# TensorE's instructions may pass at most six emitted ahead of them

## The chip, the cores and the metric

The kernel runs on one core of a Trainium2 chip as a single program. The metric is the device time of an execution in microseconds; a lower one is better. The engines are called as in the profile: PE is TensorE's matmul, PEld its weight load, DVE is VectorE, ACT is ScalarE, POOL is GpSimd and SP is SyncE.

## The reference

Two transformer-like blocks work on one sequence of 1024 positions of width 1024, all in 32-bit floats.

```
first_block:
  x = x + hybrid_mixer(rmsnorm(x))          # spatial gating, gated delta rule over 16 chunks
  x = x + memory_cross_attention(rmsnorm(x), rmsnorm(mem))
  x = x + square(relu(rmsnorm(x) @ w1)) @ w2          # 1024 -> 4096 -> 1024
  x = rmsnorm(x)
second_block:
  z = rmsnorm(x) @ w_in                               # split into nine parts
  y_pool  = windowed mean (2, 4, 8, 16) minus z, times pool_w
  y_sconv = s_b * conv3(s_c * s_h)
  y_conf  = silu(layernorm(conv31(c_a * sigmoid(c_g))))
  y_attn  = differential attention: softmax(q1 k1) - lam * softmax(q2 k2), times v
  x = x + concat(y_pool, y_sconv, y_conf, y_attn) @ w_out
  x = x + (silu(h @ w_gate) * (h @ w_up)) @ w_down    # h = rmsnorm(x)
```

## The kernel before, in words

Every product of two 32-bit matrices is made of three products of a rounded form: high times high, high times low and low times high. So each operand has two tiles, and the names end in h and l (hh and hl, wh and wl, b2h and b2l, th and tl, yh and yl). ACT makes the high tile by a copy into the rounded type; DVE, for weights POOL, makes the low tile as the difference. A PE instruction takes 128 x 128 weights against up to 512 columns. The activations stay in SBUF with features on partitions, and the weights stream in from memory as wr (or pr).

The stages follow each other: the mixer with a scan over 16 chunks (tiles pa, pb, st, vn), into which products for the memory's keys and values (gm) are woven as filling; cross attention; the first MLP; the second block's projection w_in with pooling, two convolutions and differential attention beside it; its projection w_out; the second MLP. In both MLPs the up products are made in pairs by a scheme with seven instead of eight block products; q is such a product's accumulator, b1, b2h, b2l, th and tl are its activations, ph, pl, wh, wl and p4 its weights, and pt, pu, pc and ft are what DVE and ACT make of q. fhh and fhl are the operands of the down product that follows (gm).

In the second block's projection the names are: stk, bh, bl and as for the attention's scores, amx for their maximum, ap for the softmax, apt and aT for its transpose, apo and ao for its product with v, yaT and yat for its result; tb and crb for a row spread over all partitions; cy for the 31-tap convolution; zp, pl, pld and pp for pooling (the last sum of a half is split: 64 partitions by DVE, a copy of the other 64 by POOL); gm_2301, gm_2316 and gm_2323 are output blocks of w_in, gm_2329 and gm_2361 the first two of w_out, with yh and yl from the four parts of the concatenation.

The order comes about in two steps. First the kernel itself is a set of tasks (generators). `drive` takes, at every step, the task of the best priority whose operands are ready by the kernel's own clock model, and lets it emit a few instructions. The framework's scheduler then orders each engine's instructions by a cost model of its own and adds the semaphores and the buffers' waits. The class `Eng` wraps an engine's instruction calls: it gives each instruction an ordering dependency, without a semaphore, on the one emitted a fixed number of places before it on the same engine. So the scheduler may lift an instruction over as many others at most. That number is in the table `_w` in line 203: 8 for ACT, SP and POOL, 24 for DVE. PE has no entry, so its number is 0, and its instructions may be lifted over any distance as far as their data allow. All instructions are emitted in line 210, inside that wrapper, which is why every row of the profile has line L210 and is told apart by its tiles.

Of the kernel before, what the change touches and what calls it, by code (L numbers as in the profile page):

```python
# [74 lines left out]
class Event:  # L75

    def __init__(self):
        self.done = False
        self.aps = []
# [119 lines left out]
class Eng:  # L199
    def __init__(self, eng, name, clock, tc):  # L200
        self._e, self._n, self._c, self._tc = eng, name, clock, tc
        self._past = []
        self._w = {"scalar": 8, "vector": 24, "sync": 8, "gpsimd": 8}.get(name, 0)

    def __getattr__(self, op):
        f = getattr(self._e, op)
# [2265 lines left out]
```

## Time and profile before

| what | value |
|---|---|
| time of three runs | 2617.35, 2618.58, 2618.97 us; median 2618.58 |
| profiled execution | 2613.1 us, span 2611.2 us |
| PE busy | 2499.2 us, 96% of the span, 11880 matmuls |
| DVE, ACT, POOL busy | 1563.7, 855.6, 820.5 us |
| mean granted clock of TensorE | 0.983 |

The profile comes from one execution. Busy times are added up for each engine; a wait belongs to the instruction behind it and names what ended it last. The granted clock is 1 at 2.4 GHz and 0.5 at 1.2 GHz. Times of a timeline are counted from the span's start.

### The profile page before, as it was taken

To read this page: it belongs to the slowest core of one execution; us is meant where nothing else is said; L and a number is where in the kernel's file an instruction comes from. 1 tells how busy PE (TensorE), PEld (TensorE's weight loads), DVE (VectorE), ACT (ScalarE), POOL (GpSimd) and SP (SyncE) were. 2 spreads that over 40 slices of the span, in tenths; PEclk is the share of its full clock that TensorE was granted. 3 is DMA by queue.
4 is the path that set the end of the run, shared out by engine and by line. 5 is a ranking of instruction groups with operands and counts; after the bars stand their busy time and mean duration, and the time that the engine had idled before them with its cause. 6 is when DMAs were issued, how large, how long until landed. Compare 5 with 4: busy or idle time off the path is not lost.

```text
span 2611.2 us, 30369 instructions
## 1 busy us (share of the span) xinstructions
PE 2499.2 (96%) x11880; PEld 2057.4 (79%) x11880; DVE 1563.7 (60%) x2316; ACT 855.6 (33%) x1220; POOL 820.5 (31%) x349
## 2 busy tenths in 40 slices
PE   8999999999989999999999798988989999999999
PEld 6788877888877888778888587776867888887887
DVE  7873767554457665553434857976676665664433
ACT  6422343333343333321213423434452222222210
POOL 1122121211244454322222421121245656662221
PEclk9999999999999999999999898999989999999999
DMA  3223156421132333542211232143222222236212
GB/s 130 77 77 94 63 173 207 171 89 49 65 129 82 120 105 121 227 145 99 98 57 49 97 105 57 41 145 93 85 81 73 81 89 89 65 128 235 81 49 89
DMA packets 99134, 268.25 MB, mean 103 GB/s; under 512 B 19976, under 2 KB 34480, under 8 KB 98992
## 3 DMA queue, kind: packets, MB, share of 16 engines
q1 hardware_dynamic: 78400, 192.40, 21.5%
q10 hardware_dynamic: 20592, 73.93, 8.5%
q8 instruction: 93, 1.52, 0.2%
q14 instruction: 49, 0.40, 0.1%
HBM read 196.55 MB, written 69.74 MB: 102 GB/s over the span
## 4 chain that ended last, share of the span: by engine, by line
PE 81%; DVE 11%; DMA 3%; issue 2%; ACT 2%; POOL 1%; SPq 0%; ACTq 0%; POOLq 0%; DVEq 0%
PE gm L210 46%; PE q L210 26%; DVE cy L210 1%; PE apo L210 1%; PE xs L210 1%; PE as L210 1%; PE xo L210 1%; DVE rq L210 1%; DVE ry L210 1%; DMA stk<-qkd 1%; POOL wl L210 1%; PE pk L210 1%; PE pb L210 1%; PE apt L210 1%; DVE sb L210 1%
## 5 line engine op out<-in xcount | busy, mean ns | idle before, releaser
L210 POOL TENSOR_TENSOR wl<-wr,wh 128x1024 fp32r<-128x1024 f32 (+1 forms) x137 | 339.7, 2481 | 1354.0 <-ACT wh L210 1302.2
L210 DVE TENSOR_TENSOR x<-gm,x 128x512 f32<-128x512 f32 x304 | 208.9, 688 | 346.2 <-PE gm L210 345.5
L210 ACT ACTIVATE wh<-wr 128x1024 fp32r<-128x1024 f32 (+2 forms) x147 | 153.2, 1042 | 621.7 <-PE gm L210 589.5
L210 PE MATMUL gm<-fhh,wh 128*128 128x512 f32 x864 | 337.6, 391 | 5.3 <-ACT fhh L210 4.6
L210 PE MATMUL gm<-fhl,wh 128*128 128x512 f32 x864 | 336.9, 390 | 1.0 <-DVE fhl L210 1.0
L210 PE MATMUL gm<-fhh,wl 128*128 128x512 f32 x864 | 336.6, 390 | 0.0
L210 PE MATMUL gm<-hh,wh 128*128 128x512 f32 x800 | 324.6, 406 | 11.5 <-ACT hh L210 7.3
L210 PE MATMUL gm<-hl,wh 128*128 128x512 f32 x800 | 318.3, 398 | 0.5 <-DVE hl L210 0.5
L210 PE MATMUL gm<-hh,wl 128*128 128x512 f32 x800 | 316.7, 396 | 0.0
L210 PEld LDWEIGHTS gm<-fhh,wh 128*128 128x128 f32 x864 | 162.2, 188 | 42.7 <-ACT fhh L210 5.4
L210 PEld LDWEIGHTS gm<-fhl,wh 128*128 128x128 f32 x864 | 162.3, 188 | 35.3 <-DVE fhl L210 2.2
L210 PEld LDWEIGHTS gm<-fhh,wl 128*128 128x128 f32 x864 | 162.3, 188 | 33.9
L210 PEld LDWEIGHTS gm<-hh,wh 128*128 128x128 f32 x800 | 152.9, 191 | 43.1 <-ACT hh L210 8.3
L210 PEld LDWEIGHTS gm<-hh,wl 128*128 128x128 f32 x800 | 152.7, 191 | 32.4 <-issue 0.5
L210 PEld LDWEIGHTS gm<-hl,wh 128*128 128x128 f32 x800 | 153.2, 191 | 31.4 <-DVE hl L210 1.9
L210 POOL TENSOR_TENSOR wl<-pr,wh 128x1024 fp32r<-128x1024 f32 x37 | 88.7, 2398 | 118.7 <-ACT wh L210 118.7
L210 POOL TENSOR_TENSOR wl<-sa,wh 128x1024 fp32r<-128x1024 f32 x37 | 89.1, 2409 | 107.3 <-ACT wh L210 104.3
L210 POOL TENSOR_TENSOR pl<-sb,ph 128x1024 fp32r<-128x1024 f32 x38 | 92.0, 2421 | 81.0 <-ACT ph L210 81.0
L210 PE MATMUL q<-th,wh 128*128 128x512 f32 x296 | 116.8, 395 | 0.0
L210 PE MATMUL q<-th,wl 128*128 128x512 f32 x296 | 116.3, 393 | 0.0
L210 PE MATMUL q<-tl,wh 128*128 128x512 f32 x296 | 116.2, 392 | 0.0
L210 PE MATMUL q<-th,p 128*128 128x512 f32 x304 | 103.5, 402 | 3.2 <-DVE pc L210 3.2
(461 smaller groups left out, 5233.6 us busy)
## 6 DMA issues: line engine op xcount, KB each, us to landing
fhr<-hd SPq DMA_DIRECT2D x54, 512.0 KB, 5.0
wr<-in_w_in_dram ACTq DMA_DIRECT2D x39, 512.0 KB, 3.5
xd<-x SPq DMA_DIRECT2D x32, 512.0 KB, 2.6
x<-xd SPq DMA_DIRECT2D x32, 512.0 KB, 5.4
pr<-in_ffn_w_dram SPq DMA_DIRECT2D x32, 512.0 KB, 3.6
wr<-in_ffn_w_dram ACTq DMA_DIRECT2D x32, 512.0 KB, 3.5
hd<-ft SPq DMA_DIRECT2D x27, 512.0 KB, 5.0
hd<-pc SPq DMA_DIRECT2D x27, 512.0 KB, 5.7
```

What stands on the lines that cost most here:

```text
L210: ins = f(*args, **kw)
```

## The change

One entry is added to the table of line 203, so that PE's instructions get the same ordering dependencies as those of the other engines, over six places. What is computed, the number of instructions and their emission stay as they are. The order on PE differs in 108 pieces (1454 lines of difference), on DVE in 33, on ACT in 17, on POOL in 3 and on SP in 2, since the scheduler places those engines' work by what PE does.

```diff
 class Eng:
     def __init__(self, eng, name, clock, tc):
         self._e, self._n, self._c, self._tc = eng, name, clock, tc
         self._past = []
-        self._w = {"scalar": 8, "vector": 24, "sync": 8, "gpsimd": 8}.get(name, 0)
+        self._w = {"tensor": 6, "scalar": 8, "vector": 24, "sync": 8, "gpsimd": 8}.get(name, 0)
```

The first place is on PE near the end of the second block's w_in (about 1735 to 1752 us in the trace of before): yaT are transposes of the attention's result, tb spreads the row ry, gm_2301 is an output block of 24 products. A + row stands there in the changed order, a - row only in that of before.

```order
 L210 MATMUL yaT_2302_12862<-cst_75,ao_1965_11196 128x128 x4
 L210 MATMUL yaT_2303_12868<-cst_75,ao_1965_11196 128x128 x4
+L210 MATMUL tb_2306_12882<-cst_75,ry_2273_12746 128x128 x4
+L210 MATMUL tb_2307_12889<-cst_75,ry_2273_12746 128x128 x4
 L210 MATMUL gm_2301_12858<-hh_1820_10437,wh_2248_12617 128x512
 L210 MATMUL gm_2301_12858<-hl_1821_10438,wh_2248_12617 128x512
```

Further on, at the end of gm_2301:

```order
 L210 MATMUL gm_2301_12858<-hh_1865_10683,wl_2249_12618 128x512
-L210 MATMUL as_2330_13012<-stk_2295_12841,stk_2294_12838 128x128
-L210 MATMUL as_2330_13012<-bh_1532_8648,idr_10693 128x128
-L210 MATMUL as_2330_13012<-bl_1533_8649,idr_10693 128x128
-L210 MATMUL as_2342_13049<-stk_2295_12841,stk_2294_12838 128x256
-L210 MATMUL as_2342_13049<-bh_1532_8648,idr_10693 128x256
-L210 MATMUL as_2342_13049<-bl_1533_8649,idr_10693 128x256
-L210 MATMUL tb_2306_12882<-cst_75,ry_2273_12746 128x128 x4
 L210 MATMUL gm_2316_12931<-hh_1816_10403,wh_2280_12766 128x512
-L210 MATMUL tb_2307_12889<-cst_75,ry_2273_12746 128x128 x4
 L210 MATMUL gm_2316_12931<-hl_1817_10404,wh_2280_12766 128x512
```

The two tb have moved from behind gm_2301 to ahead of it, and six score products as have gone from between the blocks gm_2301 and gm_2316 to a place behind gm_2323.

The second place is ACT at the same point of the program; wh_2313 is the high tile of a weight of w_out, crb is the evacuation of tb, wr are loads of weights. Before:

```order
L210 DMA wr_2315_12929<-in_w_out_2a_dram 128x768
L210 ACTIVATE wh_2313_12925<-wr_2282_12770 128x768
L210 ACTIVATE yat_2293_12837<-yaT_2302_12862,gv_76 128x512
L210 ACTIVATE yat_2293_12837<-yaT_2303_12868,gv_76 128x512
L210 DMA wr_2328_13009<-in_w_out_2a_dram 128x768
L210 ACTIVATE crb_2305_12881<-tb_2306_12882 128x512
L210 ACTIVATE crb_2305_12881<-tb_2307_12889 128x512
```

Now:

```order
L210 DMA wr_2315_12929<-in_w_out_2a_dram 128x768
L210 ACTIVATE yat_2293_12837<-yaT_2302_12862,gv_76 128x512
L210 ACTIVATE yat_2293_12837<-yaT_2303_12868,gv_76 128x512
L210 ACTIVATE crb_2305_12881<-tb_2306_12882 128x512
L210 ACTIVATE crb_2305_12881<-tb_2307_12889 128x512
L210 ACT_TABLE_LOAD
L210 ACTIVATE cy_2028_11573<-cy_2028_11573,gv_76 128x1024
L210 ACTIVATE cy_2240_12596<-cy_2240_12596,gv_76 128x1024
L210 ACTIVATE wh_2313_12925<-wr_2282_12770 128x768
L210 DMA wr_2328_13009<-in_w_out_2a_dram 128x768
```

wh_2313 and the load wr_2328 stood ahead of crb and the two cy, and stand behind them now.

The third place is PE at the start of the second MLP (about 1935 to 1950 us): q_2704 is the last product of the first pair, with the weight p4 as its last operand, q_2717 is the first product of the second pair and q_2718 the next.

```order
 L210 MATMUL q_2704_14439<-tl_2695_14387,p4_2605_14128 128x512
 L210 MATMUL q_2704_14439<-th_2694_14386,p4_2605_14128 128x512
+L210 MATMUL q_2717_14487<-b1_2601_14110,wh_2697_14410 128x512 x2
+L210 MATMUL q_2717_14487<-b1_2601_14110,wl_2698_14411 128x512
+L210 MATMUL q_2717_14487<-b1_2615_14158,wh_2697_14410 128x512 x2
+L210 MATMUL q_2717_14487<-b1_2615_14158,wl_2698_14411 128x512
+L210 MATMUL q_2717_14487<-b1_2633_14216,wh_2697_14410 128x512 x2
+L210 MATMUL q_2717_14487<-b1_2633_14216,wl_2698_14411 128x512
+L210 MATMUL q_2717_14487<-b1_2657_14285,wh_2697_14410 128x512 x2
+L210 MATMUL q_2717_14487<-b1_2657_14285,wl_2698_14411 128x512
 L210 MATMUL q_2718_14501<-th_2622_14182,wh_2702_14435 128x512
```

Twelve products of q_2717 (eight rows, four of them standing for two products each) stood among those of the first pair and follow it now.

## Rows read from the trace of the kernel before

**Rows 1.** Page: busy us (share of span) by engine; chain that ended last.
```profile
PE 2499.2 (96%) x11880; PEld 2057.4 (79%) x11880; DVE 1563.7 (60%) x2316; ACT 855.6 (33%) x1220; POOL 820.5 (31%) x349
...
PE 81%; DVE 11%; DMA 3%; issue 2%; ACT 2%; POOL 1%; SPq 0%; ACTq 0%; POOLq 0%; DVEq 0%
```

**Rows 2.** The waits of PE: engine, tile waiting <- releaser: us, times, longest.
```profile
PE zn L210 <- ACT zsq L210: 13.8, 1, 13.8
PE apt L210 <- DVE ap L210: 10.5, 6, 3.4
...
PE gm L210 <- DVE x L210: 4.8, 4, 1.6
...
PE pa L210 <- DVE st L210: 3.3, 3, 2.2
...
PE wsum L210 <- POOL wsT L210: 2.5, 1, 2.5
...
PE cm L210 <- DVE rq L210: 1.5, 1, 1.5
```

**Rows 3.** Windows: length, busy us of PE, PEld, DVE, ACT, POOL; granted clock; DMA share, GB/s.
```profile
1536.00:1712.00 176.00, 161.06 (x817) 135.79 (x818) 148.87 (x230) 66.88 (x132) 32.52 (x12) 0.95 0.18 57
1747.20:1789.50 42.30, 32.40 (x135) 24.41 (x135) 27.49 (x40) 19.45 (x35) 6.63 (x4) 0.88 0.53 161
```

**Rows 4.** Timeline of PE, 1747-1790: start, length, operation, [idle before <- releaser].
```profile
1749.03 0.30 PE L210 MATMUL as<-stk,stk 128*128 128x128 f32 x1 [1.80 <-DMA stk<-qkd]
...
1769.55 2.04 PE L210 MATMUL pp<-pld,wp 128*128 128x512 f32 x2 [5.50 <-DVE pld L210]
...
1784.72 0.50 PE L210 MATMUL gm<-yl,wh 128*128 128x512 f32 x1 [1.82 <-DVE yl L210]
```

**Rows 5.** Timeline of DVE, the same stretch.
```profile
1752.68 2.36 DVE L210 TENSOR_TENSOR cy<-cy,crb 128x1024 f32<-128x1024 f32 x2 [4.72 <-ACT crb L210]
...
1757.68 1.21 DVE L210 TENSOR_TENSOR pl<-pl 128x1020 f32<-128x1020 f32 x1
1763.69 0.42 DVE L210 TENSOR_REDUCE amx<-as 128x2 f32<-128x256 f32 x1 [4.80 <-PE as L210]
...
1764.22 2.82 DVE L210 TENSOR_TENSOR pl<-pl 64x1016 f32<-64x1016 f32 x1
...
1775.42 0.17 DVE L210 TENSOR_TENSOR pld<-pl,zp 128x16 f32<-128x16 f32 x1
...
1784.59 1.22 DVE L210 TENSOR_TENSOR yl<-py,yh 128x1024 fp32r<-128x1024 f32 x1
```

**Rows 6.** Timeline of ACT, the same stretch.
```profile
1747.05 0.84 ACT L210 ACTIVATE wh<-wr 128x768 fp32r<-128x768 f32 x1 [7.93 <-PE gm L210]
...
1776.30 0.37 ACT L210 ACTIVATE ap<-as,amx 128x128 f32<-128x128 f32 x1
```

**Rows 7.** Timeline of POOL, the same stretch.
```profile
1764.15 1.82 POOL L210 TENSOR_TENSOR wl<-wr,wh 128x768 fp32r<-128x768 f32 x1 [14.38 <-PE as L210]
```

**Rows 8.** Timeline of PE, start of the first MLP.
```profile
779.82 0.50 PE L210 MATMUL q<-b2h,ph 128*128 128x512 f32 x1 [4.51 <-ACT ph L210]
...
783.49 0.79 PE L210 MATMUL q<-b2h,pl 128*128 128x512 f32 x1 [1.51 <-POOL pl L210]
```

**Rows 9.** Timeline of PE, end of the first MLP's products.
```profile
1091.32 1.22 PE L210 MATMUL gm<-fhh,wh 128*128 128x512 f32 x2 [3.67 <-ACT fhh L210]
```

**Rows 10.** Timeline of DVE, the same place.
```profile
1092.44 0.68 DVE L210 TENSOR_TENSOR pc<-q,pu 128x512 f32<-128x512 f32 x1
```

**Rows 11.** Timeline of PE, end of the second MLP's products.
```profile
2351.20 0.50 PE L210 MATMUL q<-b2h,wh 128*128 128x512 f32 x1 [1.62 <-ACT pt L210]
```

**Rows 12.** Timeline of PE, start of the second MLP.
```profile
1945.00 0.50 PE L210 MATMUL q<-tl,ph 128*128 128x512 f32 x1 [0.76 <-DVE tl L210]
...
1948.96 0.80 PE L210 MATMUL q<-th,p 128*128 128x512 f32 x1 [3.22 <-DVE pc L210]
```

**Rows 13.** Timeline of DVE, the same place.
```profile
1929.93 1.23 DVE L210 TENSOR_TENSOR b2l<-xg,b2h 128x1024 fp32r<-128x1024 f32 x1 [0.72 <-ACT sq L210]
```

## The prediction

> **What bounds the kernel now.** I read the page first, then the waits of PE, then the timeline of each place where PE stands still. PE is busy for 2499.2 of 2611.2 us, 96%, and the chain that ended last is 81% PE; DVE, with 60% busy, holds 11% of that chain [rows 1]. The number of products does not change, so the change can win or lose only in the 112 us in which PE stands, in products that run at the lower clock after a stand, and nowhere else. The waits name 13.8 us at zn, 10.5 at apt, 5.5 at pp [rows 2, 4] and a tail of one to five microseconds each. A product costs 2499.2 / 11880 = 0.21 us on average [rows 1].
>
> In program order PE gets the products as the kernel's own planner emits them. The scheduler behind it then lifts products whose operands it believes to be ready past others, over any distance. From now on it may lift one over six others at most. So two things happen at each place. A product with a late operand that was lifted too far no longer stops PE there (a gain), and ready products that were lifted into a wait no longer fill it (a loss). On PE 108 pieces of the order differ. I went through the ones that lie at a wait. Negative numbers are time saved.
>
> **The pool place, 1747 to 1789: -5.** These 42.30 us hold 32.40 us of busy PE at a granted clock of 0.88 [rows 3]: PE waits 1.80 for a transfer of stk, 5.50 for pld and 1.82 for yl [rows 4]; 0.78 is left for one more wait. The 5.50 is a chain over three engines. On ACT, wh waits 7.93 us for the products of gm to give its buffer free and starts at 1747.05 [rows 6]. Behind it stand the two copies crb, for which DVE waits 4.72 us until 1752.68 [rows 5]. The pool sums on DVE come only after that; they then stand behind the score maximum amx, for which DVE waits 4.80 us until 1763.69, and the last sum of the first half takes 2.82 us [rows 5]. In the new order tb stands right behind yaT, that is ahead of the 24 products of gm_2301, wh stands behind crb and cy on ACT, and amx behind both halves of the pool on DVE.
> I follow the chain. crb is there some 4 us earlier, so cy's 2.36 us end near 1749. The first half then needs, from the rows' starts, 1752.68 + 2.36 to 1758.89 (3.9) and 1764.22 to about 1769.4, just ahead of PE's start at 1769.55 [rows 4] (5.2), less 0.7 for amx between them: 8.4 us and 0.7 for zp, so pld is ready near 1758.5. PE gets there about 1760, after its 72 products without the 1.80 wait, and the 5.50 goes. The second half ran from about 1769.4 to 1775.6 [rows 5], 6.2 us; it now starts behind gm_2323, near 1759.5, and ends near 1765.7. Then comes what was not late before: amx (1.1), the exponentials on ACT, which began at 1776.30 [rows 6], and from there to the end of the last yl at 1784.59 + 1.22 = 1785.8 [rows 5] 9.5 us of ACT and DVE. From 1766.8 that gives 1776.3. Behind the last yl PE now has the second output half, gm_2361, still to do: 18 products (3.8), 12 score products and the transposes (about 3), where before all but some of them lay in front. So the place ends at 1783.3 + 0.7 = 1784 and not at 1789.5: 5.5 saved, less half a microsecond for a product or two more at the low clock. The bounds: -9, if half of gm_2361 fits into the gap before yl as its six places allow and wl meets no sum of the pool; -1, if the chain from amx to yl grows as long as what is saved ahead of it.
>
> Of the three engines, DVE and GpSimd meet here. The 2.82 us sum runs beside wl on POOL, 1764.15 to 1765.97 [rows 5, 7]; a sum of the same size took 1.21 at 1757.68 with POOL idle [rows 5]. The Trainium skill, page SBUF — State Buffer, section "SBUF: two separate sides", calls the port pair of VectorE and GpSimd an exclusive lock that one holds for a whole instruction. The row agrees: 1.82 + 1.21 = 3.03 with a start 0.07 later and an end close to it. That rule speaks against this change, and it is a rival below.
>
> **Start of the first MLP, 776 to 790: -2 (-3.5 to 0).** PE waits 4.51 for ph and 1.51 for pl [rows 8], since ten products of q_1121 were lifted ahead of the second half of q_1116, whose operands are older. They go back behind it. The 6.0 us of waits go, but what stood ahead of them had been the filler and the next operands (pl ends on POOL near 783.5) are no earlier: a third is saved.
>
> **Ends of both MLPs' products: +1 (-0.5 to 2) and +2 (0 to 3).** At 1087.6 PE waits 3.67 for fhh [rows 9] and then runs four products of the next stage. Now the twelve products with p4 stand first. They need pc, which DVE starts at 1092.44 and ends 0.68 later [rows 10], behind fhl. So PE stands until 1093.1 and not 1091.3, and the four products (0.21 each, about 1.8 with the low clock) come after: 1.8 us of wait more, of which the four products' slower first run gives back 0.8. At 2351.20 PE waits 1.62 for pt [rows 11] after eight products that were lifted in front of it; they go behind: 8 x 0.21 = 1.7 more of wait, and 0.3 for the same pattern with pc at the end.
>
> **Start of the second MLP, 1917 to 1950: +1.5 (-1.5 to 9.3).** 23 products of four later results were lifted ahead of a product that waits for b1_2657, 4.8 us, and 12 products of q_2717 ahead of those with p4, 2.5 us. The end of this place is set by operands: tl, for which PE waits until 1945.00, and pc, for which it waits 3.22 until 1948.96 [rows 12]. b2l is ready at 1929.93 + 1.23 = 1931.2 [rows 13]. From there PE has 48 products, 48 x 0.21 = 10.1 us, or 13 with some at the low clock: 1941.3 to 1944. That is still ahead of 1945, so the 23 cost nothing. The 12 of q_2717 come after p4 and are lost, +2.5; a microsecond of earlier x from the pool place goes against it. Without the cover all 7.3 are lost, and 2 more at the low clock.
>
> **The differential attention, 1536 to 1712: 0 (-4 to +4).** The scores and transposes move back to where they are emitted. apt waits 10.5 us for ap in six places [rows 2], mostly here. But DVE is busy for 148.87 of 176 us [rows 3], with convolution taps and softmax in an order that hardly changes; PE's waits shift from one of its products to another.
>
> **Small places.** Scan (343 to 462): the wait for st, 2.2 at its longest [rows 2], gets six products as cover, others come later: -1.5 (-4 to 2). Start: the 2.5 for wsT go [rows 2], twelve products now run earlier at DVE's pace: +1 (-0.5 to 3). A projection at 680 no longer runs ahead of xt: +1 (0 to 2.5). Before zn (13.8 [rows 2]): cs and tb are a little earlier, the chain of small DVE operations that zn waits for stays: -1 (-2.3 to 1). csum stands ahead of wl on POOL, so cm's 1.5 goes [rows 2]: -1.5 (-2 to 1). One of the four waits for x, 4.8 / 4 = 1.2 [rows 2], goes: -1.2 (-1.4 to 0). All pieces that I did not follow, some ninety, can hardly gain where PE does not wait: +1.5 (0 to 8).
>
> **The sum.** -5 - 2 + 1 + 2 + 1.5 + 0 - 1.5 + 1 + 1 - 1 - 1.5 - 1.2 + 1.5 = -4.2. The profiled execution took 2613.1 us (span 2611.2 and 1.9 around it), so it would take 2608.9. The median of the three runs is 2618.58, 5.5 above the profiled one; the difference is carried to it: 2618.6 - 4.2 = 2614.4.
>
> **Rivals.**
> The gain is larger. The waits at apt and zn shrink with the order too, because DVE and ACT get their inputs in the order in which their own lists ask for them. For it: the pool place shows one engine's queue held by another's lifted product [rows 5, 6]. Against it: DVE is 85% busy in the attention [rows 3]. With -9 at the pool place and -3 in the attention the sum is -11.2: 2607.4.
> The gain is eaten by the port. In the new order wl_2314 falls on the first sums of the pool, the copy of pl on the last one, and wl_2327 on the second half. One such meeting cost 2.82 - 1.21 = 1.6 [rows 5], and the forecast has one in it; two more make the sum -4.2 + 3.2 = -1.0: 2617.6. By the skill's lock it would be nearly the same, since each holds for a whole wl of 1.82.
> Slower: PE stands at the first late operand of the second MLP. Place: 1917 to 1950. The lifted 23 + 12 products are not regained, because b2l or th come no earlier and the 48 products behind run at the low clock past 1945. Price: 9.3 in place of 1.5, and the end of the second MLP's products at its upper bound, 3 in place of 2: -4.2 + 7.8 + 1 = +4.6; with 2 more in the unfollowed pieces, which have the same pattern, +6.6, 2625.2. It decides when the 48 products end after 1945. For it: PE is the bound nearly everywhere, so every product not lifted costs its time. Against it: the row for pc shows that the end is set elsewhere.
>
> **Chances.** The forecast 0.40 (its own range 2609 to 2620), the larger gain 0.22, the port 0.15, slower 0.23. About 0.2% of the time, 5.2 us, is what a measurement can tell from no change; the line for faster is 2613.4. Half of the forecast's case lies below it: faster 0.20 + 0.22 = 0.42; same 0.20 + 0.15 = 0.35; slower 0.23. For 8 in 10 the range goes from 2604 to 2625.
>
> **What would show it.** Right: the pool place is 4 to 6 us shorter, its wait at pp is gone, and PE now waits several microseconds in front of yl; the wait for ph at 780 and that of cm for rq are gone; a wait for pc of over 4 us at 1093. Wrong: a wait at pp that stays near 5 us; more than 2 us of new wait at b1 or th near 1924 to 1945; a larger sum at apt; or a new wait in a place that I did not follow.

## The result: 1.2% slower, and where the time went

The changed kernel takes 2649.97 us (median of 4 runs, 2648.74 to 2651.66); beside it the kernel before took 2617.97. The ratio is 1.0124, with a 95% interval of [1.0111, 1.0137], and the difference 32.0 us. The forecast was 4.2 us in the other direction, with a range that ended at 2625. Here and below a difference in us is one of medians; the ratios are estimated from all runs and differ from the ratio of the medians by about 0.001 at most.

The page of the changed kernel, busy time and chain, is the answer to [rows 1]:

```profile
PE 2504.0 (95%) x11880; PEld 2062.2 (78%) x11880; DVE 1569.5 (59%) x2316; ACT 857.5 (32%) x1220; POOL 822.0 (31%) x349
...
PE 79%; DVE 13%; ACT 3%; issue 2%; DMA 2%; POOL 1%; SPq 0%; ACTq 0%; DVEq 0%; POOLq 0%
```

Its span is 2647.0 us, 35.8 more than that of the profile before. PE is busy for 2504.0, 4.8 more; it stands for 143.0 and not 112.0. So 31.0 us are standing and 4.8 are products that took longer. The chain has lost 2% of PE and gained 2% of DVE and 1% of ACT. The waits of PE (engine, waiting tile, releaser: us, times, longest) say on whom it waits; they answer [rows 2]:

```profile
PE q L210 <- ACT pt L210: 21.0, 4, 11.5
PE q L210 <- DVE pc L210: 12.0, 4, 5.4
PE zn L210 <- ACT zsq L210: 11.2, 1, 11.2
PE apt L210 <- DVE ap L210: 7.5, 1, 7.5
...
PE q L210 <- ACT b L210: 6.7, 1, 6.7
...
PE pp L210 <- DVE pld L210: 2.8, 1, 2.8
```

The first two rows have grown most. q waits 21.0 us for pt, of which there was one wait of 1.6 before [rows 11], and 12.0 for pc, of which there was 3.2 [rows 12]. What was forecast to go has gone in part: pp waits 2.8 and not 5.5 [rows 4], and cm's wait for rq is 0.6 and not 1.5 [rows 2].

I compared the starts of the same PE instructions in both traces; the table has the growth of their distance at each place. The middle column is the trace of the change; the last says what the same place did in kernels of the experiments below, bound to six there (b) or not (n). Each value comes from one profiled execution, set beside the first one of the kernel before.

| place (us in the trace before) | forecast | change | elsewhere |
|---|---|---|---|
| start, 60 to 100 | +1 | +5.4 | b +2.9 to +5.6, n -0.1 to +1.4 |
| scan and behind it, 320 to 500 | -1.5 | +2.9 | b +4.6, +7.3; n -1.4 to +1.2 |
| row factors of cross attention, 540 to 560 | none | +3.9 | b +3.9, +5.4; n 0.0 |
| projection, 680 to 700 | +1 | +4.1 | b +2.5, +4.0; n 0.0 |
| first MLP's start, 740 to 820 | -2 | +9.5 | b +8.1, +8.1; n -0.2 to +1.0 |
| first MLP's end, 1060 to 1120 | +1 | +3.1 | b +4.4, n -0.1 to +2.3 |
| bias tables, 1130 | none | +2.4 | b +0.7, n +0.2 to +3.1 |
| final norm, 1450 to 1540 | -1 | -2.6 | b -2.2 to -3.0, n -0.2 to -2.8 |
| attention, 1540 to 1710 | 0 | +2.9 | b +5.1, +7.1; n +2.5 to +6.2 |
| csum, 1710 to 1740 | -1.5 | -0.8 | b 0.0 to -1.1, n 0.0 |
| pool place and w_out, 1740 to 1880 | -6.2 | -2.7 | b -2.2 to -3.3, n -1.2 to +0.4 |
| second MLP's start, 1880 to 1990 | +1.5 | +1.3 | b +0.7, n +0.1 to -2.1 |
| second MLP's end, 2340 to 2380 | +2 | +6.7 | b +6.5, n -1.6 to 0.0 |

Between these places the distance is the same to 0.1 us over hundreds of products: from 840 to 1060 us, for example, it stays at 25.3. So the change costs nothing for each product; it costs at places. The rows on csum and the pool are parted at 1740, where both orders have done the same products: the wait of 1.80 for stk [rows 4], which goes, lies behind that point. The expectations below count up to 1750 and so put most of that gain at csum.

The largest place in full, PE first. Its rows answer [rows 8]: the start, the length, and in brackets the wait ahead and its releaser.

```profile
776.82 0.50 PE L210 MATMUL gm<-xoh,wh 128*128 128x512 f32 x1 [0.97 <-ACT wh L210]
...
779.25 0.79 PE L210 MATMUL gm<-xoh,wl 128*128 128x512 f32 x1 [1.70 <-POOL wl L210]
...
795.65 0.50 PE L210 MATMUL q<-b,wh 128*128 128x512 f32 x1 [0.52 <-DVE b L210]
...
807.89 0.80 PE L210 MATMUL q<-b2h,wh 128*128 128x512 f32 x1 [11.51 <-ACT pt L210]
```

PE waits for the last block's weights (0.97 and 1.70), which lifted products of q had filled before; then, behind the b products of its first result, for 11.51 us. It waits for pt: the copy by which ACT saves the first half of the sum of q, before PE adds the second half in the same bank. ACT's list at that time:

```profile
798.05 1.06 ACT L210 ACTIVATE wh<-sa 128x1024 fp32r<-128x1024 f32 x1 [1.89 <-DVE sa L210]
803.65 1.06 ACT L210 ACTIVATE ph<-sb 128x1024 fp32r<-128x1024 f32 x1 [4.54 <-DVE sb L210]
804.61 0.61 ACT L210 ACTIVATE p<-pr 128x512 fp32r<-128x512 f32 x1
805.13 1.13 ACT L210 ACTIVATE xg<-x,gv 128x1024 f32<-128x1024 f32 x1
806.30 1.06 ACT L210 ACTIVATE b2h<-xg 128x1024 fp32r<-128x1024 f32 x1
807.26 0.58 ACT L210 ACTIVATE pt<-q 128x512 f32<-128x512 f32 x1
```

pt could have been copied at 796.4, when its products were done; it stands behind ph, which waits 4.54 for sb, and behind three more. DVE tells why sb is late:

```profile
787.92 0.69 DVE L210 TENSOR_TENSOR tb<-xg,xg 128x512 f32<-128x512 f32 x1 [11.34 <-PE gm L210]
788.53 2.88 DVE L210 TENSOR_TENSOR tb<-xg,ta 128x512 f32<-128x512 f32 x1
...
800.19 2.82 DVE L210 TENSOR_TENSOR sb<-pr,pr 128x512 f32<-128x512 f32 x1
802.94 0.68 DVE L210 TENSOR_TENSOR sb<-pr,sa 128x512 f32<-128x512 f32 x1
```

tb waits until 787.92 for PE. In the kernel before, the same operation started at 762.26. Of the 25.7 us between the two, 15.8 are the loss of the earlier places; the other 9.9 are new:

```profile
762.26 1.70 DVE L210 TENSOR_TENSOR tb<-xg,xg 128x512 f32<-128x512 f32 x1 [1.48 <-PE gm L210]
```

Its operands xg come from ACT, so what it waits for is not a result of PE's but a buffer that PE reads last. At 762.2 PE had just run two products of gm_1082 that had been lifted over 22 others; the second is the last reader of a tile xol, whose place in SBUF this tb takes. In the new order they stand behind the whole of gm_1080. That shifts tb, th, the next xg and b, and at last sb, which now meets wl on POOL and takes 2.82 us instead of 0.68:

```profile
799.19 3.28 POOL L210 TENSOR_TENSOR wl<-sa,wh 128x1024 fp32r<-128x1024 f32 x1 [4.13 <-ACT wh L210]
```

At the second MLP's end ACT's list is again what PE waits for. The ACT rows:

```profile
2378.23 0.33 ACTq L210 DMA_DIRECT2D wr<-in_w_down_a_dram  x1
2378.61 1.06 ACT L210 ACTIVATE pc<-pc 128x1024 f32<-128x1024 f32 x1 [5.61 <-POOL p L210]
2379.57 0.58 ACT L210 ACTIVATE pt<-q 128x512 f32<-128x512 f32 x1
```

and those of PE, which answer [rows 11]:

```profile
2380.20 0.80 PE L210 MATMUL q<-b2h,wh 128*128 128x512 f32 x1 [3.39 <-ACT pt L210]
...
2397.49 0.79 PE L210 MATMUL q<-th,p 128*128 128x512 f32 x1 [3.25 <-DVE pc L210]
```

The load stands in ACT's list ahead of pc and pt; ACT is idle for 5.61 us until POOL is done with p, and only then come the load, pc and pt. PE's 3.39 had been 1.62, with eight products of q in front; the 3.25 for pc had been covered by products of gm. At the first MLP's end it is pc alone, as forecast, 5.40 us, and on DVE (second fence, which answers [rows 10]) pc starts as soon as fhl is done:

```profile
1119.88 0.79 PE L210 MATMUL q<-th,p 128*128 128x512 f32 x1 [5.40 <-DVE pc L210]
```

```profile
1117.99 1.23 DVE L210 TENSOR_TENSOR fhl<-fhr,fhh 128x1024 fp32r<-128x1024 f32 x1 [2.07 <-ACT fhh L210]
1119.14 0.68 DVE L210 TENSOR_TENSOR pc<-q,pu 128x512 f32<-128x512 f32 x1
```

### The profile page after: what moved, and what is told of

The parts are those of the page before. It is cut to its first block, busy times and chain, and to the rows that moved or that the text cites. A ratio compares the mean times of both kernels' runs of the same rounds, so it can differ in the third digit from the quotient of the medians.

```text
span 2647.0 us, 30367 instructions
## 1 busy us (share of the span) xinstructions
PE 2504.0 (95%) x11880; PEld 2062.2 (78%) x11880; DVE 1569.5 (59%) x2316; ACT 857.5 (32%) x1220; POOL 822.0 (31%) x349
## 4 chain that ended last, share of the span: by engine, by line
PE 79%; DVE 13%; ACT 3%; issue 2%; DMA 2%; POOL 1%; SPq 0%; ACTq 0%; DVEq 0%; POOLq 0%
PE gm L210 45%; PE q L210 25%; DVE cy L210 2%; PE as L210 1%; DVE csc L210 1%; PE apo L210 1%; PE xo L210 1%; PE xs L210 1%; DVE rp L210 1%; POOL wl L210 1%; PE pb L210 1%; DVE rq L210 1%; PE pk L210 1%; DVE ry L210 1%; DVE amx L210 1%
```

## The experiments

All that bind PE's order at some places only use one edit in the wrapper: the entry for tensor holds where the number in the name of the product's result lies in a list. That splits the change cleanly: inside the listed ranges PE's order is that of the changed kernel, elsewhere that of the kernel before (in one kernel, `[(1059, 1120)]`, three results just behind the range move along).

```diff
+ON = [...]
 ...
-            if self._w:
+            on = self._w
+            if self._n == "tensor":
+                k = int(args[0].tensor.name.split("_")[1])
+                on = self._w if any(a <= k < b for a, b in ON) else 0
+            if on:
```

**Edges of the MLPs alone, and all but them.**

```diff
+ON = [(1059, 1155), (1430, 1500), (2540, 2760), (3100, 3180)]
```

> The bound of six holds only at the starts and ends of the two MLPs' pair products; everywhere else PE's order is that of the kernel before. Theory 'filling': the loss is made place by place, where products that had been lifted over more than six others had filled a wait. Then the places add up as the changed kernel's trace showed them: first MLP's start +9.5, its end +5.5, second MLP's start +1.3, its end +6.7, together +23.0, so about 2641 us beside 2618, and no drift in between. Rival 'price of the bound': the order itself, by more waits on semaphores or by other engines' changed orders, costs over the whole program; then these four places give less than half of 32, under 16 us.

Measured: 2635.33 beside 2617.09, ratio 1.0080 [1.0064, 1.0096], +18.2 us, where +23.0 had been expected.

```diff
+ON = [(0, 1059), (1155, 1430), (1500, 2540), (2760, 3100), (3180, 9999)]
```

> The complement: the bound of six holds everywhere but at those four places. 'Filling': 35.8 of the trace less 23.0, that is +12.8 us, about 2631; the pool place keeps its gain of some 3 us, and the start (60 to 90 us) its loss of 5.5. 'Price of the bound': more than 16 us, 2634 or above.

Measured: 2631.99, ratio 1.0063 [1.0047, 1.0080], +14.9 us. The two add to 33.1, against 32.0 for the whole, with intervals of about 4 us on each: the loss is made place by place. The times of the second kernel alone don't tell the two theories apart (12.8 and over 16 had been expected); the distance that stays the same between the places does. The edges alone are over half of the loss, though less than the 23.0 that the difference of two profiles gave; one reason is seen with the second profile below.

**The places that had gained.**

```diff
+ON = [(1860, 1936), (2240, 2510)]
```

> The bound of six holds only where the changed kernel's trace was ahead: the final norm's end of the first block with zn (about 1456 to 1535 us) and the stretch from csum over the pool place to w_out (1712 to 1893). 'Filling' (each place by itself): -2.6 and -2.7, about 2613, the fastest of all. 'Price of the bound': no gain, 2618 or more. A third possibility: the gains were only made because earlier places had run late (weights and transfers were then further ahead of PE), and vanish alone: 2618.

Measured: 2613.57, ratio 0.9992 [0.9978, 1.0006]: -3.5 us by the medians, and by its interval no difference that can be told. In its trace nothing is gained at csum and 2.3 us at the pool place. That gain is the order's: the whole stretch from 1710 to 1880 is 2.4 to 4.4 us shorter in all four kernels that are bound to six over it, and at most 1.2 shorter in those whose order there is that of before. What was seen at the final norm can't be put down to the change, since kernels with an unchanged order there go from -0.2 to -2.8 as well.

**A bound of 48.**

```diff
-        self._w = {"tensor": 6, "scalar": 8, "vector": 24, "sync": 8, "gpsimd": 8}.get(name, 0)
+        self._w = {"tensor": 48, "scalar": 8, "vector": 24, "sync": 8, "gpsimd": 8}.get(name, 0)
```

> The same table with 48 in place of 6, over the whole program. The order is then that of before at the scan, the projection at 680, the ends of both MLPs and the norm; it differs at the start (55 places of the order, 66 with six), a little at the first MLP's start (10 in place of 68), in the attention and at the pool place. 'Filling': +5.5 at the start, +1 at the first MLP, -1 to -3 at the pool place: +2 to +5, about 2622. 'Price of the bound': the dependencies are as many as with six, so most of the 32 us stay.

Measured: 2610.98 beside 2617.09, ratio 0.9982 [0.9970, 0.9994], -6.1 us by the medians and -4.7 by the ratio; faster than both kernels, where a small loss had been expected. There are as many ordering dependencies as with six, so the dependencies are not what costs. What differs is how much is forbidden. The dependency binds an instruction only to the one six or 48 places before it, so the number is no strict bound, but it comes close: in the order of before 675 matmuls stand ahead of ones emitted earlier and pass up to 99 of them; with 48 there are 595, passing up to 44; with six there are 96, passing up to 8. Once more, on another chip:

> The bound of 48 once more, beside the next kernel. It was 6.1 us faster than before, [1.6, 7.9], where +2 to +5 had been expected. If that holds, -4 to -8 again; if it was the spread of that chip, within 2 us of before.

Measured: 2609.99 beside 2616.56, ratio 0.9977 [0.9967, 0.9987], -6.6 us. It holds. Its PE waits:

```profile
PE zn L210 <- ACT zsq L210: 13.1, 1, 13.1
PE apt L210 <- DVE ap L210: 12.0, 6, 6.0
...
PE q L210 <- ACT ph L210: 3.6, 1, 3.6
...
PE q L210 <- ACT pt L210: 2.4, 2, 1.6
```

pt is waited for 2.4 us in two places, against 21.0 in four with six and one wait of 1.62 before [rows 11]: 48 places let most products of a pair pass each other as before. ph is waited for 3.6 and not 4.5 us [rows 8], apt somewhat longer, 12.0 for 10.5 [rows 2]. None of this is a gain of 6 us; both profiles of this kernel came from its longer runs (2615.48 and 2616.12), so they can't show where it lies.

**Where the gain of 48 sits.** For each range its own bound:

```diff
+ON = [(1860, 1936, 6), (1936, 2240, 48), (2240, 2300, 6), (2300, 2760, 48)]
```

> Each part of the second block with the bound that looked best in the traces: 6 at the final norm's end and around csum, 48 in the attention, the pool place, w_out and the second MLP's start, none elsewhere (so the whole first block keeps its order, with the start where 48 differs from before). If the gains are those of csum (-2.3), of the pool place and of the order with 48 there: -6 to -8, 2609, no slower than with 48 everywhere. Rival: the gain of 48 is at the start of the program, where 55 places differ; then this kernel gains 2 to 3 us at most.

Measured: 2611.71, ratio 0.9988 [0.9977, 1.0000], -4.9 us by the medians and -3.1 by the ratio. That is 1.7 us less than with 48 everywhere, which the spread of the two (12.0 and 14.5 us between shortest and longest run) doesn't separate, and it lies between the expectation and the rival's two to three. So neither is shown: where the gain of 48 sits and what makes it stay open.

**The kernel before, a second time.**

> The kernel before once more, for a second profile of it: how far two profiles of the same order differ, place by place. If the end of the first MLP (1060 to 1140 us) and the attention (1540 to 1710) are stable, they stand within 0.5 us of the first profile, and the +2 to +4 us that kernels with an unchanged order there have shown is a cost of the change elsewhere; if not, it is the transfers' own spread, and about 3 of the changed kernel's 5.5 us at the first MLP's end remain.

Measured: span 2617.5, 6.3 us more than the first profile of the same order. It agrees with that to about 1 us up to 1120, grows by 3.1 at the bias tables, where PE waits for a load, and by 4.9 in the attention, and wins back 1.0 at the pool place:

```profile
1131.10 0.71 PE L210 MATMUL pbt<-tf,cst 128*128 128x256 f32 x2 [3.11 <-DMA tf<-bd]
```

The same wait was 1.64 in the first profile. Much of the rest is the clock: the windows of both places (columns as in [rows 3]) have a granted clock of 0.89 and 0.84 in the second profile,

```profile
1125.00:1140.00 15.00, 11.89 (x46) 9.38 (x45) 7.51 (x9) 6.26 (x9) 2.40 (x1) 0.89 0.65 218
1695.00:1716.00 21.00, 18.24 (x86) 15.23 (x85) 19.46 (x31) 8.35 (x13) 3.40 (x1) 0.84 0.20 71
```

and of 1.00 in the first:

```profile
1125.00:1140.00 15.00, 13.36 (x59) 10.76 (x58) 9.93 (x12) 6.39 (x9) 2.40 (x1) 1.00 0.72 261
1695.00:1716.00 21.00, 19.51 (x116) 16.48 (x116) 19.58 (x35) 9.10 (x14) 4.54 (x2) 1.00 0.21 76
```

The first profile of before was one of its shorter executions (2613.1; 31 runs of the last series lie from 2612.71 to 2627.64). So the +2.4 and +2.9 of the table at these two places, and some 3 us of what the edges were expected to cost, can't be put down to the change. The first MLP's end is doubtful too: the second profile agrees with the first there, but kernels with an unchanged order lose up to 2.3 us.

**The start alone.**

```diff
+ON = [(0, 200)]
```

> The bound of six only for the first 100 us (the start of the mixer with decays and transposes kT). 'Filling': +5.5 as in the two traces that had it, 2622.5. Rival: at the start nothing is bound by PE yet (the first weights have just come), and the loss is regained in the scan, where DVE sets the pace: within 2 us, up to 2619.

Measured: 2620.46 beside 2615.99, ratio 1.0018 [1.0008, 1.0028], +4.5 us; in its trace +5.5 by 100 us, and +0.8 more over the scan. Nothing is regained there. Not all of the 5.5 is the order, though. The last kernel below has the same order of PE up to here and the same four waits (1.72, 0.28, 0.69 and 2.37 us), and lost 2.9: its 32 products pe took 3.71 us together and the eight kT behind the last wait 1.09, against 5.03 and 1.97 in the changed kernel. From 65 to 69 us and from 82 to 86 the granted clock was 1.00 in the former and 0.57 in the latter.

**The first MLP's start, apart.** Three kernels; first only the blocks ahead of it and the first result:

```diff
+ON = [(1059, 1120)]
```

> The bound of six only for the last two blocks of the projection ahead of the first MLP and the first result of its first pair; the later results of that pair may be lifted as before. 'Filling': what the seven lifted products of that first result had covered was the wait for the weights wh and wl of the last block, 0.97 + 1.70, and the low clock behind it: +3 to +5 us; the ten lifted products of the next result still fill the wait for pt, so the other half of this place's 9.5 is not lost. 2620 to 2622. Rival: the first result's late place is what makes x and sb late; then nearly all of 9.5 comes, 2625 or more.

Measured: 2624.19 beside 2615.99, ratio 1.0032 [1.0020, 1.0044], +8.2 us, in its trace +5.3. The lifted products of the next result wait for ph themselves, now 8.4 us and not 4.5:

```profile
PE q L213 <- ACT ph L213: 8.4, 1, 8.4
```

The median lies between the two expectations, and neither account was right: filling with ten products is no help when they wait for the same late sb, and something ahead of ph had become late. The trace named it, the wait of tb. Two kernels tell it apart: the whole place, and the same without gm_1082.

```diff
+ON = [(1059, 1155)]
```

> The bound of six only at the first MLP's start (the last two blocks of the projection ahead of it and the first pair). By the trace of the changed kernel +9.5 us: about 2625.5 beside 2616, with the wait of 11.5 for pt. It is the partner of the next kernel.

```diff
+ON = [(1059, 1082), (1083, 1155)]
```

> The same, but the last block of the projection, gm_1082, is not bound. In the order that gives, two of its products (with xoh_824 and xol_825) stand ahead of the rest of gm_1080, as before; every product of the pair stays in strict order. 'Buffer': those two products were the last readers of xol_825, and tb, which DVE starts at 787.92 after 11.34 us of waiting for PE in the changed kernel and at 762.26 after 1.48 in the kernel before, waits for that buffer. With them in front, tb starts some 9 us earlier, sb is no longer late, pt comes about 9 us after the end of gm_1082 as before and not 15, and the wait for pt falls from 11.5 to about 6: some 5 us of the 9.5 go, 2620 to 2621. Rival 'filling' alone: two products are 0.5 us of work, so no more than 1 us is won, 2624.5 or more.

Measured: 2622.27 beside 2616.56, ratio 1.0025 [1.0014, 1.0036], +5.7; and 2618.28, ratio 1.0007 [0.9996, 1.0018], +1.7; both 2 to 3 us below what had been expected. The two intervals just overlap, so the pair rests on the traces, in which the place costs 8.1 and 3.0 us. PE's order differs in those two products and nothing else. DVE's tb and sb and PE's wait of the first kernel, in two fences:

```profile
770.33 0.69 DVE L213 TENSOR_TENSOR tb<-xg,xg 128x512 f32<-128x512 f32 x1 [9.97 <-PE gm L213]
...
782.61 2.82 DVE L213 TENSOR_TENSOR sb<-pr,pr 128x512 f32<-128x512 f32 x1
```

```profile
790.31 0.79 PE L213 MATMUL q<-b2h,wh 128*128 128x512 f32 x1 [11.50 <-ACT pt L213]
```

and of the second:

```profile
760.97 1.71 DVE L213 TENSOR_TENSOR tb<-xg,xg 128x512 f32<-128x512 f32 x1 [1.47 <-PE gm L213]
...
777.72 0.68 DVE L213 TENSOR_TENSOR sb<-pr,pr 128x512 f32<-128x512 f32 x1
```

```profile
783.28 0.79 PE L213 MATMUL q<-b2h,wh 128*128 128x512 f32 x1 [6.51 <-ACT pt L213]
```

tb waits for PE 1.47 us and not 9.97, sb takes 0.68 and not 2.82, and PE's wait for pt falls from 11.50 to 6.51. Two products, half a microsecond of work, move 5.0 us of wait. So it was what they gave free, the buffer, and not the filling; what makes the 3.0 that are left, no run parts further.

**pt out of ACT's list**, in the changed kernel with its bound of six:

```diff
-            nc.scalar.activation(t[:, :512], a[0], AF.Copy)
+            if first or not more:
+                nc.vector.tensor_copy(t[:, :512], a[0])
+            else:
+                nc.scalar.activation(t[:, :512], a[0], AF.Copy)
```

> The changed kernel, with the copy of the first pair product pt out of PSUM made by DVE and not by ACT in the first and the last pair of each MLP. 'Late operand': in the changed kernel PE waits there 21.0 us in 4 places for pt, which stands in ACT's list behind work that waits for DVE (ph for sb) or behind a load (at 2378). On DVE it stands right behind sb (802.94 + 0.68) and behind pc at 2374.7. So pt comes 3.6 us earlier at the first MLP's start and 4.8 at the second's end, with what the low clock cost there, and some at the two others: 8 to 12 us faster than the changed kernel, 2638 to 2642. Rival 'number of products': PE would stand for the next operand anyhow, since too few products are left to it; then less than 3 us is won, 2647 or more.

Measured: 2638.44 beside 2615.99, ratio 1.0084 [1.0065, 1.0103]; 22.4 over before, where the changed kernel has 32.0 in its own series: 9.6 us are won, with intervals of 5.0 and 3.4 us on the two. PE's wait for pt:

```profile
PE q L210 <- DVE pt L210: 11.5, 2, 7.9
```

11.5 us in two places for 21.0 in four. In the trace the first MLP's start costs 6.0 and not 9.5, the second's end 1.3 and not 6.7. The 3.6 and 5.4 us of these two places are most of the 9.6. So the place of pt in a list is about a third of the loss, and not that there are too few products. At the second MLP's end PE's order is the same in both kernels; at the two starts it changes a little with the edit.

## Why the prediction was wrong

**What held.** The mechanism of the slower rival, PE standing at a late operand with nothing lifted into the wait, is what happened; 0.23 went to it, it was put at the second MLP's start, where +1.5 was forecast and +1.3 came, and its price (+6.6 in all) was too low by a factor of five. The attention's 0 holds within the spread. Of cm's wait, 1.48 before, 0.56 is left (forecast -1.5 for csum, measured -0.8). The first MLP's end has the wait for pc that was forecast, 5.40 at 1119.88.

**The premise.** That "the change can win or lose only in the 112 us in which PE stands" and in products behind a stand left out the time in which PE did not stand because a lifted product ran. Standing grew from 112.0 to 143.0 us, and much of it in places that had no wait, or a small one, before.

**First step that failed: the first MLP's start, -2.** "PE waits 4.51 for ph and 1.51 for pl ... a third is saved" read the two waits that stood there, and took the order behind them to be free. The first result's second half waits for pt, and pt stands last in ACT's list behind ph, in the kernel before as well; with ph and pl gone from PE's way the same sb was waited for one step later. And the chain to sb was taken as given ("the next operands ... are no earlier"), while tb became 9.9 us later by a buffer. In place of -2 the place cost +8.1 to +9.5.

**Second: the pieces not followed, +1.5, and the small places at +1.** The start, the row factors of cross attention and the projection cost 5.4, 3.9 and 4.1, and the scan, forecast at -1.5, cost 2.9. Each of the first three has the pattern that the forecast had priced at the MLPs' ends, short operations of DVE or ACT under which lifted products ran. The waits did not exist in the trace before, or were 0.24 us long, because they were covered, so a reading that started from the waits passed them by. The rows of the changed kernel show them open, at 82, 555 and 696 us:

```profile
82.35 1.97 PE L210 MATMUL kT<-cst,cy 128*128 128x128 f32 x8 [2.37 <-ACT cy L210]
```

```profile
555.14 1.06 PE L210 MATMUL tb<-cst,ry 128*128 128x128 f32 x8 [2.76 <-DVE ry L210]
```

```profile
696.03 0.30 PE L210 MATMUL xt<-cst,xp 128*128 128x128 f32 x1 [2.52 <-DVE xp L210]
```

Each is followed by a stretch at the low clock or by products that had been in front: 11 of gm_986 at 696. In the scan, too, a wait of 2.99 us stands open at 353.78, of vT for cy on ACT, in all three kernels bound to six there; no run takes it apart further.

**Third: the ends of the MLPs, +1 and +2.** The waits were right in kind, and a size was off: +3.1, of which up to 2.3 may be spread, and +6.7. The second adds the wait for pt (1.8 more), that for pc (3.25, forecast 0.3) and the low clock behind both: the granted clock is 0.75 over the 26.6 us from 2376.4, where it had been 0.91 over the 20.0 from 2349.

**Fourth: the pool place, -5 and -1.2.** The waits for stk, 1.80, and for the first pld, 5.50, are gone, as forecast [rows 4]; PE waits for the second pld instead, and then 0.5 to 1.1 us at each yh and yl:

```profile
1797.49 1.95 PE L210 MATMUL pp<-pld,wp 128*128 128x512 f32 x4 [2.85 <-DVE pld L210]
```

Its sums now meet POOL four times. Two of them, with what POOL did:

```profile
1781.30 1.69 DVE L210 COPY pl<-pl 128x2 f32<-128x2 f32 x1
...
1785.55 2.06 DVE L210 TENSOR_TENSOR pl<-pl 64x1016 f32<-64x1016 f32 x1
...
1792.17 1.68 DVE L210 COPY pl<-pl 64x2 f32<-64x2 f32 x1
```

```profile
1780.06 2.90 POOL L210 TENSOR_TENSOR wl<-wr,wh 128x768 fp32r<-128x768 f32 x1 [14.66 <-ACT wh L210]
1785.50 1.04 POOL L210 COPY pl<-pl 64x1024 f32<-64x1024 f32 x1 [2.54 <-DVE pl L210]
1790.94 2.88 POOL L210 TENSOR_TENSOR wl<-wr,wh 128x768 fp32r<-128x768 f32 x1 [4.40 <-ACT wh L210]
```

The two small copies took 1.69 and 1.68 us and end when wl ends; the 2.06 us sum ran beside the copy of pl, with [rows 5] at 1.21 for one alone. In the trace before the first of these copies took a tenth of that:

```profile
1756.27 0.17 DVE L210 COPY pl<-pl 128x2 f32<-128x2 f32 x1
```

That was the rival of the port. By the Trainium skill (SBUF — State Buffer, section "SBUF: two separate sides") of a VectorE operation that needs the pair of ports shared with GpSimd and an operation of GpSimd, the one that starts first keeps the pair until it is done, and the other is blocked. The trace agrees: both copies end 0.03 us after POOL's wl. Behind the last yl the second output half was then left, as the forecast said. Of 6.2 us 2.7 came. The 3.5 that are missing are close to the 3.2 that the rival asked for two more meetings, but no run takes POOL away from these sums, so that this is the reason is argued and not shown.

## What to carry to other kernels

Before you bound how far a scheduler may move work, look for what its moves cover: a wait that is hidden leaves no row, so go through the moved instructions and ask for each what ran beneath it, which bank or buffer it gave free, and whose list stands behind that buffer. A copy out of an accumulator on which the next product waits belongs on an engine whose list is not held by a load or by another engine. And a bound need not be tight: 48 places, which forbid only the far moves, gave 5 to 6 us, by a cause that no run here shows, and six lost 32.

## What the runs showed that was not expected

One execution of the same order can be 6 us longer than another by two places, 3.1 us at a wait for a load (1.64 and 3.11 us at the bias tables) and 4.9 in the attention, both with a lower granted clock, and agree to about 1 us over the first 1120 us. A difference of two profiles is therefore read by places, and a place that differs by as much in kernels with the same order there tells nothing. And the two products that moved 5 us of wait were 0.5 us of work.
